# Down projection by seven products: another order of the products, one weight sum for each, and low parts on VectorE

## Chip, cores, metric

One core of one Trainium2 chip runs the whole kernel. The metric is device time in microseconds (us); the median of three runs is given. Numbers of the profile come from one profiled execution.

## The reference

One encoder layer over 1024 tokens of width 1024 in float32: a modulated norm, one input projection into an attention group and an mLSTM group, an output projection, then the feed-forward part with 2816 hidden units and a final norm. What matters here is the end:

```python
h = modulate(rms_norm(x, norm_ffn_g[l]), sh2, sc2)
ffn = (jax.nn.silu(h @ w_gate[l]) * (h @ w_up[l])) @ w_down[l]
x = x + g2[:, None, :] * ffn
...
return rms_norm(x, final_norm_g)
```

The change lies in `@ w_down[l]`, a product of 1024 x 2816 by 2816 x 1024.

## The kernel before

**Precision.** Each float32 operand is split into a high part (rounded to the type fp32r by ScalarE) and a low part (the operand minus its high part). A product is three matmuls, high by high, low by high, high by low (`mm3`, lines 312 to 314 of the profile).

**Seven products for eight.** Weights and activations are cut in halves in two directions, and the block product is made with seven products and some sums (Winograd's form of Strassen's scheme). The hidden units are 22 blocks of 128, taken as NP = 11 pairs `p`. `WD[c, p]` holds the rows of block 2p + c of `w_down`, 128 x 1024; its column halves give the weight quarters a11 = `WD[0, p]` left, a21 = `WD[0, p]` right, a12 = `WD[1, p]` left, a22 = `WD[1, p]` right. The activation side of each product `m` (11, 21, T2, T3, T1, 22, T4) has been summed already in the stage before and lies in DRAM as `act_d[p][m]`, 128 x 512. Product `m` runs over the 11 pairs; for each it multiplies one 128 x 512 weight piece (four output blocks of 128) with one activation piece, into four PSUM accumulators. T4 is done in two halves of 256 tokens. When a product ends, `finish` adds its four accumulators, scaled by the gate g2, into those quarters of the residual that the table `CELLS` names: four for 11, one for 21, three for T2, two each for T3 and T1, one each for 22 and T4, so 16, 4, 12, 8, 8, 4 and 4 (twice, half as wide) additions on VectorE. `FINAL` says after which product a quarter is complete, so that its squares for the final norm can be taken.

**Weight pieces.** `load_w` makes the weight piece of one product and pair, one call per pair, four ahead. For T2 it makes three sums: a11 - a21 in place of a11, s = a22 - a11 in a tile of its own, and, after the split, a12 - s in place of a12. T3 then finds its weight in a11 and 22 its own in a12; T1 adds a22 to a21 in place. The high part `wch` is ScalarE's, the low part `wcl` VectorE's, in four buffers each. T4's weight a22 is split into a tile `a`. The first KB = 5 pairs of product 11 load their weights as pieces instead (below).

**Pieces.** Activation pieces (and those five weight pieces) come through `load_piece`: SyncE issues a load into one of three buffers `wst`; ScalarE makes `whi`, then the engine chosen in `split` makes `wlo`; the buffer is free after that. `split` uses GpSimd (`gps`) unless `lo` names VectorE. In the down projection `lo` is `dve` only for the second half of T4. Loads, x and `wd` rows share SyncE's queue, which is served in order.

**Order.** Each engine runs its instructions in the order of the program. That order is made while the program is written out: `ck` is a model of the engines' times, in which a `chain` of steps puts each step behind what it waits for. VectorE's instructions for sums, low parts and accumulators so interleave as the model's times say.

Of the kernel before, what the change touches and what calls it, by code (L numbers as in the profile page):

```python
# [11 lines left out]
F32 = mybir.dt.float32  # L12
# [8 lines left out]
P = 128  # L21
# [3 lines left out]
HALF = 512  # L25
# [23 lines left out]
MIX = [("o", i) for i in range(16)] + [("m", (i + 8) % 16) for i in range(16)]  # L49
FF = [("b", p) for p in range(NB)] + [("v", 0)] + [("s", (p, i)) for p in range(1, NP - 1) for i in range(2)] + [("v", NP - 1)]  # L50
SET = ["A11", "A12", "S2", "S3", "S1", "A22", "S4"]
DOWN = ["11", "21", "T2", "T3", "T1", "22", "T4"]

VEC = {}
_o = 0
# [194 lines left out]
def layer_kernel(ctx, tc, xT, c, w_ada, vecs, cons, rope, w_f, w_fT, w_t0, w_t, w_o, w_gu, w_d, out):  # L250
# [43 lines left out]
    x1_d = [dram.tile([P, S], F32, name=f"x1_d{i}") for i in range(KT)]  # L294
    act_d = [{m: dram.tile([P, HALF], F32, name=f"act_d{p}{m}") for m in DOWN} for p in range(NP)]

# [24 lines left out]
    def halves(n):  # L321
        return slice(n * HALF, (n + 1) * HALF)

    ck = Clock()
    dve, act, gps = Engine(ck, nc.vector, "dve"), Engine(ck, nc.scalar, "act"), Engine(ck, nc.gpsimd, "gps")
# [39 lines left out]
    with tc.manual_schedule():  # L365
# [48 lines left out]
        def down_w():  # L414
            out = []
            for m in DOWN:
                for c in range(2 if m == "T4" else 1):
# [10 lines left out]
        specs = [first[f][b] for b in range(2) for f in range(3)]  # L428
        start = {("t", 0): [6, 8, 9, 11], ("q", 1): [7, 10]}
# [31 lines left out]
        def split(p, delay, src, shape, *before, lo=None):  # L461

            def split_hi():
                p[0] = lined("whi", shape)
                act.activation(p[0], src(), AF.Copy)

            def split_lo():
                p[1] = lined("wlo", shape)
                (lo or gps).tensor_sub(p[1], src(), p[0].bitcast(F32))

            ck.chain(delay, *before, split_hi, split_lo, flag=p[2])
# [3 lines left out]
        def piece(i):  # L475

            p = [None, None, Flag()]
            made.append((p, Flag(), []))
            if not isinstance(specs[i][0], str):
                src, n, ncol = specs[i][:3]  # L480

                def arrived(st, arrive):
                    made[i][2].append(st)
                    ck.chain(arrive, lambda: None, flag=made[i][1])

                raw([P, n, ncol], src, p[2], arrived)

        def load_piece():

            i = len(pieces)  # L490
            if i == len(specs):
                return
            while len(made) <= min(i + (AHEAD if i + AHEAD >= start["down"] else 0), len(specs) - 1):
                piece(len(made))
            p, there, st = made[i]
            pieces.append(p)
            if isinstance(specs[i][0], str):
                set_piece(p, *specs[i][1])
                return
            split(p, 0.0, lambda: st[0], [P, *specs[i][1:3]], there,  # L500
                  lo=dve if specs[i][3:] == (1,) or i < 9 or start["o", 0] <= i < start["b", 1] else None)

        def weights(w0, k, per):
            w = pieces[w0[k // per] if isinstance(w0, list) else w0 + k // per]
# [88 lines left out]
        def issue():  # L593

            kind, i = loads[0][0], int(loads[0][1:] or 0)
            del loads[0]
            if kind == "x":
                ck.chain(dma(x_t[i], xT[i]), lambda: None, flag=x_at[i])
            elif kind == "a":
                ada_load(i)  # L600
            else:
                load_piece()
            if loads:
                ck.at(max(0.0, ck.dma_t - 5.0 - ck.now), issue)
# [760 lines left out]
        HB, b22_ok, rs_used = {}, {}, []  # L1365
        hb_ok = {(m, k): Flag() for m in DOWN for k in range(4)}

# [84 lines left out]
        def set_piece(e, p, i, m):  # L1452

            s = 2 * p + i
            R, Q = RAW[s], set_s[s]
            set_p[s][m] = e[2]
            eng = dve if p == 0 else gps
            done = lambda x: [set_p[s][x]] if x in set_p[s] else []
            sh = [P, 4, P]
            if m[0] == "A":  # L1460
                split(e, 0.0, lambda: R[m[1:]][0], sh, R[m[1:]][1], lo=eng)
            elif m == "S2":
                split(e, 0.0, lambda: Q[2], sh, s2_ok[s], lo=eng)
            elif m == "S3":
                split(e, 0.0, lambda: R["11"][0], sh, s2_ok[s], *done("A11"),
                      lambda: dve.tensor_sub(R["11"][0], R["11"][0], R["21"][0]), lo=eng)
            elif m == "S1":
                split(e, 0.0, lambda: Q[1], sh, s2_ok[s], lo=eng)
            else:
                split(e, 0.0, lambda: R["12"][0], sh, s2_ok[s], R["12"][1], *done("A12"),  # L1470
                      lambda: dve.tensor_sub(R["12"][0], R["12"][0], Q[2]), lo=eng)
            if len(set_p[s]) == (7 if p >= NB else 5):
                ck.chain(0.0, *set_p[s].values(), lambda: None, flag=sets_done[s])
                if s + 2 < 2 * NP:
                    ck.chain(0.0, sets_done[s], lambda: load_raws(s + 2))
# [159 lines left out]
        def act_sums(p):  # L1635
# [6 lines left out]
            def new(m, a, b):  # L1642
# [9 lines left out]

        CELLS = {"11": ("11", "12", "21", "22"), "21": ("11",), "T2": ("12", "21", "22"), "T3": ("21", "22"),
                 "T1": ("12", "22"), "22": ("12",), "T4": ("21",)}
        FINAL = {"21": "11", "T1": "22", "22": "12", "T4": "21"}
        WD, wd_ok = {}, {(c, p): Flag() for c in range(2) for p in range(NP)}
        x1_ok = {(k, n): Flag() for k in range(KT) for n in range(NH)}
        wseq = [(m, c, p) for m in DOWN for c in range(2 if m == "T4" else 1) for p in range(NP)
                if m != "11" or p >= KB]
        WE = {q: [None, None, Flag()] for q in wseq}  # L1660
# [31 lines left out]
        def load_w():  # L1692
            if not wseq:
                return
            q = m, c, p = wseq.pop(0)
            e = WE[q]
            if m == "T4":
                if c == 0:
                    t = pb.tile([P, 2, HALF], F32R, tag=f"wd0{p}", name="a22")
                    e[:2] = t[:, 0], t[:, 1]  # L1700
                    WE[m, 1, p] = e
                    a22 = WD[1, p][:, halves(1)]
                    ck.chain(0.0, lambda: act.activation(t[:, 0], a22, AF.Copy),
                             lambda: dve.tensor_sub(t[:, 1], a22, t[:, 0].bitcast(F32)), flag=e[2])
                return
            a11, a12, a21, a22 = (WD[x, p][:, halves(r)] for r in range(2) for x in range(2))
            src = {"11": a11, "21": a12, "T3": a11, "T1": a21, "22": a12, "T4": a22}.get(m)
            ok = [wd_ok[x, p] for x in ((0,) if m in ("11", "T3") else (1,) if m in ("21", "22", "T4") else (0, 1))]
            steps, rest = [], []
            if m == "T2":  # L1710

                src = pb.tile([P, HALF], F32, tag="s", name="s", bufs=5)
                if ("11", 0, p) in WE:
                    ok.append(WE["11", 0, p][2])
                ok.append(WE["21", 0, p][2])
                steps = [lambda: dve.tensor_sub(a11, a11, a21), lambda: dve.tensor_sub(src, a22, a11)]
                rest = [lambda: dve.tensor_sub(a12, a12, src)]
            elif m in ("T3", "22"):
                ok.append(WE["T2", 0, p][2])
            elif m == "T1":  # L1720
                ok.append(WE["T3", 0, p][2])
                steps = [lambda: dve.tensor_add(a21, a21, a22)]
            eng = dve

            def hi():
                e[0] = pb.tile([P, HALF], F32R, tag="wch", name="wch", bufs=4)
                act.activation(e[0], src, AF.Copy)

            def lo():
                e[1] = pb.tile([P, HALF], F32R, tag="wcl", name="wcl", bufs=4)  # L1730
                eng.tensor_sub(e[1], src, e[0].bitcast(F32))

            ck.chain(0.0, *ok, *steps, hi, lo, *rest, flag=e[2])

        def down():
            i = start["down"]
            flat = lambda t: t.rearrange("p a b -> p (a b)")
            for m in DOWN:
                for c in range(2 if m == "T4" else 1):
# [28 lines left out]
        def finish(m, c, banks):  # L1768
            w = 256 if m == "T4" else HALF
            for o in range(4):  # L1770
# [11 lines left out]
                ck.chain(LAT, opened3, *steps, flag=f)  # L1782
                cell = FINAL.get(m)
                if cell in ("12", "22"):
# [476 lines left out]
        pb = ctx.enter_context(tc.tile_pool(name="pb", bufs=1))  # L2261
# [81 lines left out]
```

## Time and profile before

| | |
|---|---|
| median of 3 runs | 1366.47 us (1365.18 to 1368.64) |
| the profiled execution's own time | 1367.06 us |
| its span, first to last instruction | 1365.0 us |
| mean granted TensorE clock | 0.977 |
| TensorE busy | 1282.9 us, 94% |
| VectorE busy | 1052.8 us, 77% |
| ScalarE busy | 708.7 us, 52% |
| GpSimd busy | 644.5 us, 47% |
| down projection, first to last matmul start | 1123.74 to 1353.24 us |

In rows of the profile PE is TensorE, PEld its weight loads, DVE VectorE, ACT ScalarE, POOL GpSimd, SP SyncE. L98 is a helper's line through which all engine instructions pass, so tiles tell them apart, written out<-in. A busy TensorE is not a TensorE at full pace, since matmuls overlap; distances between starts tell more.

### The profile page before, as it was taken

Reading aid. Unit: us, or ns where it says so; the run is one execution under the profiler, and the core shown is the slowest. Engines: PE = TensorE matmul, PEld = TensorE weight load, DVE = VectorE, ACT = ScalarE, POOL = GpSimd, SP = SyncE. Lnnn points to the kernel's source line nnn. Section 1 sums busy time; section 2 is a strip of 40 time slices with the busy share of each in tenths; the row PEclk is TensorE's granted clock in tenths of the full one; section 3 lists DMA queues with packets and bytes.
Section 4 is the critical chain, followed back from the end, with each engine's and each line's share of the span. In section 5 each row is a group of like instructions: output and inputs, shape, how many; then the busy total and the mean of one; then the engine's idle time right before and its main releaser. Section 6 shows DMA issues by size and latency. Waiting matters only on the chain.

```text
span 1365.0 us, 19568 instructions
## 1 busy us (share of the span) xinstructions
PE 1282.9 (94%) x6596; PEld 1077.1 (79%) x6596; DVE 1052.8 (77%) x1601; ACT 708.7 (52%) x1342; POOL 644.5 (47%) x536
## 2 busy tenths in 40 slices
PE   7899888899999989999999999999999999979997
PEld 5787676888788979788778788888888887858887
DVE  7936698976689847989789989867666754898866
ACT  6575466778577855555577422333323334444462
POOL 0352577655665524444124155554545445545542
PEclk9888898999999999999999999999999999989999
DMA  9444333233233226773553344332333259623314
GB/s 360 159 122 138 113 103 97 78 104 110 67 92 103 76 83 192 235 248 109 186 178 115 99 144 150 118 108 100 109 107 116 72 187 347 252 80 104 100 59 158
DMA packets 104467, 187.02 MB, mean 137 GB/s; under 512 B 11568, under 2 KB 33200, under 8 KB 104368
## 3 DMA queue, kind: packets, MB, share of 16 engines
q1 hardware_dynamic: 90976, 163.68, 37.2%
q10 hardware_dynamic: 13392, 22.10, 4.3%
q8 instruction: 52, 0.85, 0.3%
q14 instruction: 47, 0.39, 0.1%
HBM read 139.33 MB, written 42.73 MB: 133 GB/s over the span
## 4 chain that ended last, share of the span: by engine, by line
PE 60%; DVE 18%; issue 7%; DMA 5%; ACT 5%; POOL 4%; SPq 1%; DVEq 0%; ACTq 0%; POOLq 0%
PE acc L312 16%; PE acc L314 16%; PE acc L313 16%; DVE sst L98 3%; DVE y L98 3%; DVE PT L98 2%; PE av L1210 2%; DVE x L98 2%; PE T L1191 2%; PE S L1159 1%; POOL wlo L98 1%; DMA wst<-act_d 1%; DMA wst<-in_w_gu_dram 1%; DVE wd L98 1%; DVE s L98 1%
## 5 line engine op out<-in xcount | busy, mean ns | idle before, releaser
L98 POOL TENSOR_TENSOR wlo<-wst,whi 128x512 fp32r<-128x512 f32 (+2 forms) x165 | 239.9, 1460 | 287.7 <-ACT whi L98 234.0
L98 ACT ACTIVATE whi<-wst 128x512 fp32r<-128x512 f32 (+2 forms) x223 | 133.6, 605 | 119.6 <-PE acc L314 28.3
L313 PE MATMUL acc<-x,whi 128*128 128x512 f32 x352 | 136.9, 389 | 0.0
L98 POOL TENSOR_SCALAR P<-P,sst 128x1024 f32<-128x1024 f32 x64 | 85.9, 1343 | 89.5 <-DVE sst L98 65.4
L98 POOL TENSOR_TENSOR wlo<-wr,whi 128x512 fp32r<-128x512 f32 x52 | 72.2, 1389 | 71.7 <-ACT whi L98 68.6
L312 PE MATMUL acc<-hh,whi 128*128 128x512 f32 x224 | 98.1, 438 | 6.9 <-ACT xp L98 5.2
L312 PE MATMUL acc<-whi,wch 128*128 128x512 f32 x244 | 96.0, 394 | 5.2 <-ACT wch L98 5.2
L314 PE MATMUL acc<-whi,wcl 128*128 128x512 f32 x244 | 96.5, 396 | 3.2 <-DVE wcl L98 3.2
L313 PE MATMUL acc<-wlo,wch 128*128 128x512 f32 x244 | 96.1, 394 | 0.5 <-POOL wlo L98 0.4
L98 ACT ACTIVATE P<-S,sst,colq 128x1024 f32<-128x1024 f32 x64 | 77.2, 1207 | 36.8 <-DVE sst L98 27.3
L313 PE MATMUL acc<-hl,whi 128*128 128x512 f32 x224 | 91.0, 406 | 0.0
L314 PE MATMUL acc<-hh,wlo 128*128 128x512 f32 x224 | 90.7, 405 | 0.0
L98 DVE TENSOR_TENSOR PT<-T,PT 128x512 fp32r<-128x512 f32 x128 | 83.3, 680 | 9.5 <-ACT PT L98 9.3
L98 ACT ACTIVATE whi<-wr 128x512 fp32r<-128x512 f32 x56 | 35.4, 632 | 100.1 <-DVE wr L98 48.3
L98 DVE TENSOR_REDUCE sst<-S 128x1 f32<-128x1024 f32 x64 | 77.7, 1213 | 12.5 <-PE S L1159 12.4
L1191 PE MATMUL T<-ident,P 128*128 128x128 f32 x512 | 72.6, 280 | 15.3 <-DVE PT L98 10.5
L98 ACT ACTIVATE PT<-T 128x512 fp32r<-128x512 f32 x128 | 71.7, 596 | 29.1 <-PE T L1191 28.3
L312 PE MATMUL acct<-whi,hh 128*128 128x256 f32 (+1 forms) x256 | 81.5, 318 | 4.5 <-ACT hh L98 3.1
L1191 PEld LDWEIGHTS T<-ident,P 128*128 128x128 f32 x512 | 59.3, 143 | 26.2 <-issue 9.7
L98 DVE TENSOR_TENSOR wcl<-wd,wch 128x512 fp32r<-128x512 f32 x50 | 50.0, 1012 | 37.9 <-ACT wch L98 29.4
L98 POOL TENSOR_TENSOR wlo<-s,whi 128x512 fp32r<-128x512 f32 x40 | 55.1, 1379 | 49.4 <-ACT whi L98 49.4
L1210 PE MATMUL av<-PT,va 128*128 128x256 f32 x512 | 71.4, 287 | 7.0 <-DVE PT L98 6.9
(486 smaller groups left out, 3849.4 us busy)
## 6 DMA issues: line engine op xcount, KB each, us to landing
wr<-in_w_gu_dram SPq DMA_DIRECT2D x66, 256.0 KB, 2.8
ada<-in_w_ada_dram SPq DMA_DIRECT2D x64, 256.0 KB, 3.4
wd<-in_w_d_dram SPq DMA_DIRECT2D x22, 512.0 KB, 6.7
wst<-in_w_gu_dram SPq DMA_DIRECT2D x42, 256.0 KB, 2.9
wst<-act_d SPq DMA_DIRECT2D x33, 256.0 KB, 4.4
ada<-in_w_ada_dram SPq DMA_DIRECT2D x16, 512.0 KB, 7.2
wst<-in_w_o_dram SPq DMA_DIRECT2D x32, 256.0 KB, 3.3
act_d<-sg ACTq DMA_DIRECT2D x29, 256.0 KB, 2.0
```

The source lines that it names most:

```text
L98: return fn(*args, **kw)
L312: nc.tensor.matmul(acc, w[0], x[0], start=first, stop=False)
L313: nc.tensor.matmul(acc, w[0], x[1], start=False, stop=False)
L314: nc.tensor.matmul(acc, w[1], x[0], start=False, stop=last)
L1159: nc.tensor.matmul(sp[:, halves(n)], qs[:, j * P:(j + 1) * P], k2[g][m][:, halves(n)], start=m == 0, stop=m == 1)
L1191: nc.tensor.transpose(tp[:, k], Pt[q][:, (4 * b + k) * P:(4 * b + k + 1) * P], ident)
L1210: nc.tensor.matmul(av, va[:, k, h // 4], PT[it][m][:, k], start=(k, m) == (0, 0), stop=(k, m) == (NJ - 1, 1))
```

## The change

The order of the products becomes 11, 21, T3, T1, T2, 22, T4. Each of T3, T1, T2 and 22 makes its weight by one sum in place: T3 a11 - a21 in a11; T1 a21 + a22 in a21; T2 a22 - a11 in a11 (after T3 is done with it); 22 a12 - a11 in a12 (after T2). The tile s goes. Quarter 22 is complete after T2. All low parts of pieces of the down projection are made by VectorE.

```diff
-DOWN = ["11", "21", "T2", "T3", "T1", "22", "T4"]
+DOWN = ["11", "21", "T3", "T1", "T2", "22", "T4"]
...
-                  lo=dve if specs[i][3:] == (1,) or i < 9 or start["o", 0] <= i < start["b", 1] else None)
+                  lo=dve if i >= start["down"] or i < 9 or start["o", 0] <= i < start["b", 1] else None)
...
-        FINAL = {"21": "11", "T1": "22", "22": "12", "T4": "21"}
+        FINAL = {"21": "11", "T2": "22", "22": "12", "T4": "21"}
...
-            src = {"11": a11, "21": a12, "T3": a11, "T1": a21, "22": a12, "T4": a22}.get(m)
+            src = {"11": a11, "21": a12, "T3": a11, "T1": a21, "T2": a11, "22": a12}[m]
             ok = [wd_ok[x, p] for x in ((0,) if m in ("11", "T3") else (1,) if m in ("21", "22", "T4") else (0, 1))]
-            steps, rest = [], []
-            if m == "T2":
-
-                src = pb.tile([P, HALF], F32, tag="s", name="s", bufs=5)
+            steps = []
+            if m == "T3":
                 if ("11", 0, p) in WE:
                     ok.append(WE["11", 0, p][2])
-                ok.append(WE["21", 0, p][2])
-                steps = [lambda: dve.tensor_sub(a11, a11, a21), lambda: dve.tensor_sub(src, a22, a11)]
-                rest = [lambda: dve.tensor_sub(a12, a12, src)]
-            elif m in ("T3", "22"):
-                ok.append(WE["T2", 0, p][2])
+                steps = [lambda: dve.tensor_sub(a11, a11, a21)]
             elif m == "T1":
                 ok.append(WE["T3", 0, p][2])
                 steps = [lambda: dve.tensor_add(a21, a21, a22)]
+            elif m == "T2":
+                ok.append(WE["T3", 0, p][2])
+                steps = [lambda: dve.tensor_sub(a11, a22, a11)]
+            elif m == "22":
+                ok += [WE["T2", 0, p][2], WE["21", 0, p][2]]
+                steps = [lambda: dve.tensor_sub(a12, a12, a11)]
...
-            ck.chain(0.0, *ok, *steps, hi, lo, *rest, flag=e[2])
+            ck.chain(0.0, *ok, *steps, hi, lo, flag=e[2])
```

More of the change, by code (lines that the diff above doesn't have):

```diff
@@ L1722, in load_w @@
                 steps = [lambda: dve.tensor_add(a21, a21, a22)]
-            eng = dve
+            elif m == "T2":
[4 more added lines that the diff above has]
+                steps = [lambda: dve.tensor_sub(a12, a12, a11)]
             def hi():
@@ L1730, in lo @@
                 e[1] = pb.tile([P, HALF], F32R, tag="wcl", name="wcl", bufs=4)
-                eng.tensor_sub(e[1], src, e[0].bitcast(F32))
-            ck.chain(0.0, *ok, *steps, hi, lo, *rest, flag=e[2])
+                dve.tensor_sub(e[1], src, e[0].bitcast(F32))
+            ck.chain(0.0, *ok, *steps, hi, lo, flag=e[2])
         def down():
```

## The prediction

> **What bounds the kernel now.** I read the page for the span, then the trace's busy time by stage with the cuts laid where TensorE begins a new product of the down projection (found in its timeline: 132 matmuls a product, 11 pieces x 4 output blocks x 3 terms; the last product has two halves of 132 narrower ones).
>
> ```profile
> span 1365.0 us, 19568 instructions
> ...
> core 0: us, PE busy (x) PEld busy (x) DVE busy (x) ACT busy (x) POOL busy (x), PEclk, DMA share, GB/s
> 1123.74:1156.05 32.31, 31.15 (x133) 24.40 (x132) 11.96 (x16) 13.28 (x21) 16.48 (x13) 1.00 0.92 328
> 1156.05:1186.34 30.29, 30.26 (x133) 24.66 (x132) 26.50 (x33) 13.88 (x23) 16.31 (x12) 1.00 0.83 320
> 1186.34:1227.88 41.54, 33.53 (x133) 25.43 (x132) 40.19 (x45) 18.56 (x34) 19.56 (x14) 0.92 0.27 77
> 1227.88:1258.88 31.00, 30.56 (x134) 24.63 (x132) 26.06 (x29) 12.72 (x22) 16.90 (x13) 1.00 0.38 110
> 1258.88:1288.80 29.92, 29.92 (x134) 24.78 (x132) 26.02 (x28) 12.82 (x22) 15.48 (x11) 1.00 0.33 97
> 1288.80:1318.72 29.92, 29.92 (x134) 24.78 (x132) 21.53 (x30) 16.31 (x31) 13.05 (x11) 1.00 0.23 68
> 1318.72:1335.40 16.68, 16.68 (x136) 16.20 (x135) 14.57 (x18) 10.99 (x22) 8.79 (x8) 1.00 0.26 85
> 1335.40:1353.24 17.84, 17.84 (x143) 17.58 (x142) 12.33 (x27) 5.62 (x15) 2.50 (x3) 1.00 0.63 207
> ```
>
> The rows are products 1 to 6 and the two halves of product 7. Products 5 and 6 run without a gap: 29.92 us, or 0.227 us a matmul. Against that, product 1 (11) loses 2.4 us, product 2 (21) 0.4, product 3 (T2) 11.6, product 4 (T3) 1.1: 15.5 us in all. That sum is the ceiling of what any relief of the feeding engines can give here. In product 3 VectorE is busy 40.19 of 41.54 us (97%) and the clock granted to TensorE falls to 0.92. TensorE's timeline shows how:
>
> ```profile
> 1194.28 0.39 PE L314 MATMUL acc<-whi,wcl 128*128 128x512 f32 x1
> 1198.85 0.50 PE L312 MATMUL acc<-whi,wch 128*128 128x512 f32 x1 [4.18 <-ACT wch L98]
> 1199.18 0.56 PE L313 MATMUL acc<-wlo,wch 128*128 128x512 f32 x1
> 1202.51 0.79 PE L314 MATMUL acc<-whi,wcl 128*128 128x512 f32 x1 [2.77 <-DVE wcl L98]
> 1203.10 0.63 PE L312 MATMUL acc<-whi,wch 128*128 128x512 f32 x1
> 1203.53 0.63 PE L313 MATMUL acc<-wlo,wch 128*128 128x512 f32 x1
> ```
>
> TensorE waits for the high part wch and then the low part wcl of one weight piece, and then goes on at 0.43 us a matmul, half its pace, for a while: the pause is paid twice. Behind wch stands VectorE, as the waits between engines and the groups of VectorE's instructions in product 3 say:
>
> ```profile
> ACT wch L98 <- DVE s L98: 25.5, 9, 4.2
> ...
> L98 DVE TENSOR_TENSOR s<-wd,wd 128x512 f32<-128x512 f32 x9 | 12.1, 1347 | 0.0
> L98 DVE TENSOR_TENSOR wd<-wd,s 128x512 f32<-128x512 f32 x10 | 8.9, 900 | 0.0
> L98 DVE TENSOR_TENSOR wcl<-s,wch 128x512 fp32r<-128x512 f32 x9 | 8.3, 926 | 1.2 <-ACT wch L98 1.2
> L98 DVE TENSOR_TENSOR wd<-wd 128x512 f32<-128x512 f32 x9 | 8.3, 925 | 0.0
> ```
>
> Three sums and one low part a piece, by those means 1.35 + 0.90 + 0.93 + 0.93 = 4.1 us, where TensorE needs 29.92/11 = 2.72 us a piece. VectorE is what product 3 is bound by. Why the same instruction costs 0.9 to 1.35 us on average is seen by laying its single rows beside GpSimd's:
>
> ```profile
> 1208.91 1.69 POOL L98 TENSOR_TENSOR wlo<-wst,whi 128x512 fp32r<-128x512 f32 x1 [1.82 <-ACT whi L98]
> 1214.28 1.29 POOL L98 TENSOR_TENSOR wlo<-wst,whi 128x512 fp32r<-128x512 f32 x1 [3.68 <-ACT whi L98]
> ...
> 1211.67 0.68 DVE L98 TENSOR_TENSOR wd<-wd,s 128x512 f32<-128x512 f32 x1
> 1212.28 0.68 DVE L98 TENSOR_TENSOR s<-wd,wd 128x512 f32<-128x512 f32 x1
> 1212.88 0.68 DVE L98 TENSOR_TENSOR wd<-wd 128x512 f32<-128x512 f32 x1
> 1214.32 1.80 DVE L98 TENSOR_TENSOR s<-wd,wd 128x512 f32<-128x512 f32 x1
> ```
>
> Between GpSimd's two low parts VectorE starts an instruction every 0.60 to 0.61 us (call it 0.605). The one that starts 0.04 us after GpSimd's at 1214.28 takes 1.80: it sat out the 1.29. The price of a VectorE instruction with two tile inputs is thus 0.605 us alone and up to 1.8 beside GpSimd.
>
> **The change, part by part.**
>
> *Low parts moved from GpSimd to VectorE.* Over products 1 to 7a:
>
> ```profile
> L98 POOL TENSOR_TENSOR wlo<-wst,whi 128x512 fp32r<-128x512 f32 x66 | 93.2, 1419 | 94.4 <-ACT whi L98 91.5 <-PE acc L314 2.6
> L98 POOL TENSOR_TENSOR wlo<-wst,whi 128x256 fp32r<-128x256 f32 x11 | 10.5, 962 | 8.5 <-ACT whi L98 8.5
> ...
> L98 DVE TENSOR_TENSOR wcl<-wd,wch 128x512 fp32r<-128x512 f32 x50 | 50.0, 1012 | 37.9 <-ACT wch L98 29.4 <-DMA wd<-in_w_d_dram 8.3
> ```
>
> GpSimd loses 93.2 + 10.5 us; beyond its two multiplications of the first closing norm nothing is left on it before 1335 us. VectorE gains 66 x 0.605 + 11 x about 0.35 (half width, half of 0.605 and a little) = 44 us, and should get back what it waits for GpSimd: of the 50 low parts in the last row alone 50 x (1.012 - 0.605 - the 0.08 by which a row's 0.68 overlaps the next start) = 16 us, and the sums and low parts of the group rows above (0.90 to 1.35) the like. So its total hardly moves; what matters is how it falls on the products.
>
> *One sum a product.* T2's three sums become one each in T3, T2 and 22, T1 keeps its own: 44 sums before and after. With the low parts, products 3 to 5 now ask VectorE for 33 instructions at 0.605 = 20.0 us, plus the additions out of the accumulators that the product before leaves. These are
>
> ```profile
> L98 DVE SCALAR_TENSOR_TENSOR x<-acc,mod,x 128x512 f32<-128x512 f32 x52 | 35.5, 737 | 0.7 <-PE acc L314 0.7
> ...
> 1155.74 4.04 DVE L98 SCALAR_TENSOR_TENSOR x<-acc,mod,x 128x512 f32<-128x512 f32 x6
> ```
>
> six in 4.04 us, about 0.66 apart (one tile input, the other in the accumulator; I see no such row stretched like the sums). In the order 11, 21, T3, T1, T2, 22 the products leave 16, 4, 8, 8, 12 and 4. VectorE's bill: product 2: 22 x 0.605 + 16 x 0.66 = 23.9 us; 3: 20.0 + 2.6 + three norm sums 1.8 = 24.4; 4 and 5: 20.0 + 5.3 = 25.3; 6: about 27 full instructions (7 sums, 7 low parts of 22, 8 of T4's weights, 5 of pieces) 16.3, 6 half ones 2.1, 12 additions 7.9, 3 norm sums 1.8 = 28.1; TensorE takes 29.92 each time. Before, VectorE at 26.06 and 26.02 us in products 4 and 5 cost TensorE little or nothing, so 24 to 25 should pass. Product 3 then goes from 41.54 to about 30.2: -11.3. Product 4, whose 1.1 us is the tail of the same backlog: -1.1. Product 6 is at 94%, with four weight pieces (10.9 us of TensorE) made ahead: I put +0.5, bounds 0 and +3. Product 7 (VectorE 14.57 of 16.68 in its first half; the half-width low parts add some 3 us, the low parts of T4's weights give as much back): +0.5, bounds 0 and +3.
>
> *Product 1.* Its stalls hang on GpSimd's low parts, which also free the three load buffers. The chain there, merged rows of which every other kind is left out:
>
> ```profile
> 1126.58 1.78 POOL wlo L98
> ...
> 1132.02 1.31 POOL wlo L98
> ...
> 1140.28 1.30 POOL wlo L98
> ...
> 1152.07 1.27 POOL wlo L98
> ...
> 1153.38 0.50 PE acc L313
> ```
>
> Four links of 1.3 to 1.8 us would be 0.7 each: up to 2.9 us sooner, of which 2.4 are TensorE's stall. But DMA is busy at 0.92 in product 1's row of the table, so part turns into waiting for loads: -1.4, bounds 0 and -2.4. VectorE's own queue costs nothing new here: ScalarE makes the high parts of both kinds in one queue already, so the low parts come in the order that VectorE now gets.
>
> *Product 2.* Here a cover goes. At 1153.38 TensorE takes a piece whose low part ended at that moment: the pieces have no lead. And 16 additions stand on VectorE from 1155.74, six in a row. GpSimd took a low part beside them:
>
> ```profile
> 1155.84 1.30 POOL L98 TENSOR_TENSOR wlo<-wst,whi 128x512 fp32r<-128x512 f32 x1 [1.26 <-ACT whi L98]
> ```
>
> On VectorE it can stand behind some of them: behind all six it would end at about 1160.4, where TensorE wants that piece (the second of the product) at 1156.05 + 2.72 = 1158.8, a stall of 1.6, and SyncE's load that waits for the buffer, with the weight rows queued behind it, starts 3.2 us later; two or three times over, 5 us. At best low parts get cheaper and the 0.4 goes: bounds -0.4 and +5. Up to four additions can be queued at one time, one per accumulator, so a wait of 1 to 2 us is nearer: +1.0.
>
> *No cost:* removing the tile s, the moved final cell 22 (still the fifth product's), the last product and the closing norm (same instructions, 11.8 us behind 1353.24).
>
> Sum: -1.4 + 1.0 - 11.3 - 1.1 + 0.5 + 0.5 = -11.8 us. The profiled execution took 1367.06 us (span 1365.0 and 2.06 around it), 0.6 above the median of 1366.47; the difference carries over: 1366.47 - 11.8 = 1354.7.
>
> **A rule weighed.** The Trainium skill, "Perfetto Trace Analysis", section Optimizing Scalar/DVE Operations, advises to take work off a saturated VectorE, even to GpSimd, and adds that between those two it may not help as they share a read port. By its first half, at the 97% of product 3, this change would go the wrong way; by its second it may pay. "SBUF — State Buffer", section Who interferes with whom, makes the second half definite: a VectorE instruction with two SBUF inputs and a GpSimd instruction that reads SBUF lock each other out for a whole instruction. The 1.80 us row beside GpSimd's 1.29 agrees; by it the sum is the -11.8 above, by the first half alone it is the second rival below.
>
> **The rivals.**
>
> *The second product pays.* The piece low parts stand behind the additions by their worst (+5), and products 6 and 7 cost +2 more than I put: -11.8 + 4 + 2, about 1360.5. For it: no lead, 16 additions, and loads that hang on the low part. Against: 23.9 of 29.92 us, and only TensorE's third product needs those accumulators.
>
> *VectorE becomes the bound (slower).* If the slow instructions are not GpSimd's doing, VectorE's prices stay at the means: 1.012 and 0.737. Then products 2 to 6 take 22 x 1.012 + 11.8 = 34.1; 36 x 1.012 + 2.9 = 39.3; twice 33.4 + 5.9 = 39.3; about 33 x 1.012 + 8.8 = 42.2: 194 us against 162.7 before, +31 less 1.4, about 1396. It decides at a mean of (162.7 - 48 x 0.66)/157 = 0.83 us for the 157 instructions; from there on the kernel is slower. Against: every run of 0.6 us starts lies where GpSimd is idle.
>
> *The stall only moves.* The third product waits for something else, the weight rows above all, of which the last are loaded late:
>
> ```profile
> wd<-in_w_d_dram SPq DMA_DIRECT2D x22, 512.0 KB, 6.7
> ...
> 1174.00 0.43 SPq L317 DMA_DIRECT2D wd<-in_w_d_dram  x1
> ```
>
> The last one lands near 1181, and it is for the fifth piece, due at 1186 + 4 x 2.72 = 1197: 16 us to spare. It would take all of that and more to eat the gain: 1366.
>
> **How the numbers follow.** A change within 0.3% (4.1 us, about what a measurement can tell here) is "same". Forecast, 1351 to 1358.5: 0.67. Second product pays, 1358.5 to 1362.4: 0.18. All 15.5 us gone, 1351.0 or less: 0.04. Stall moves: 0.06. VectorE the bound: 0.05. Faster 0.89, same 0.06, slower 0.05. The range 1351.0 to 1361 holds the forecast and most of the second case, 0.81.
>
> **What the profile after would show.** Right: no row of low parts on GpSimd in the down projection, VectorE's two-input means near 0.68 us, product 3 (now T3) near 30 us with granted clock 1.00, VectorE at 80 to 95% in products 2 to 6 all the same. Product 2 longer than 30.3 us with waits of TensorE for wlo: the second rival. Means above 0.83 us with GpSimd idle: the third. The prediction is wrong if weight pieces come late in product 3 though VectorE has idle time ahead of them, or if product 6 or 7 stalls by more than 3 us.

## The result, and the profile after

The changed kernel takes 1357.72 us (median of 8 runs, 1349.35 to 1361.06), the kernel before 1365.66 us (8 runs, 1361.64 to 1369.61): ratio 0.9933, 95% interval 0.9917 to 0.9949. It is faster by 0.7%, inside the range of the prediction, by 8 us where 11.8 were forecast.

The profiled execution took 1354.44 us, by the first line of its page with

```profile
span 1352.7 us, 19570 instructions
```

Its busy time by stage, cut again where TensorE begins a product (132 matmuls each, the last in two halves):

```profile
core 0: us, PE busy (x) PEld busy (x) DVE busy (x) ACT busy (x) POOL busy (x), PEclk, DMA share, GB/s
1119.56:1152.58 33.02, 30.64 (x133) 24.44 (x132) 18.22 (x28) 13.79 (x22) 0.00 (x0) 1.00 0.89 316
1152.58:1184.94 32.36, 30.34 (x133) 24.81 (x133) 28.23 (x46) 15.20 (x25) 0.00 (x0) 1.00 0.89 321
1184.94:1214.86 29.92, 29.92 (x134) 24.77 (x132) 25.26 (x42) 17.12 (x30) 0.00 (x0) 1.00 0.41 107
1214.86:1244.78 29.92, 29.92 (x134) 24.77 (x132) 25.67 (x43) 12.92 (x22) 0.00 (x0) 1.00 0.35 98
1244.78:1274.70 29.92, 29.92 (x134) 24.77 (x132) 25.67 (x43) 12.92 (x22) 0.00 (x0) 1.00 0.34 97
1274.70:1305.56 30.86, 30.25 (x134) 24.70 (x132) 30.20 (x52) 16.65 (x31) 0.00 (x0) 1.00 0.23 68
1305.56:1322.24 16.68, 16.68 (x136) 16.20 (x135) 12.81 (x23) 10.04 (x19) 2.62 (x2) 1.00 0.24 72
1322.24:1340.93 18.69, 18.60 (x143) 17.70 (x142) 13.71 (x28) 6.58 (x17) 3.27 (x4) 1.00 0.59 205
```

The third product, 41.54 us before, runs at TensorE's pace with the full granted clock. The fourth lost its 1.1 us. Products 1, 2, 6 and 7 are longer than before, by 0.7, 2.1, 0.9 and 0.9 us. From the first to the last matmul start the down projection takes 221.4 us against 229.5: 8.1 us less, close to the difference of the medians (7.9). The two profiled executions differ by more, 12.6 us, because the down projection began 4.2 us sooner in this one. That is not the change's doing: in the 14 profiled executions of this study it began anywhere from 1117.5 to 1124.4 us, and two more executions of this same kernel began it at 1122.1 and 1120.2.

VectorE's groups over products 1 to 7a, then all that GpSimd does there:

```profile
L98 DVE TENSOR_TENSOR wlo<-wst,whi 128x512 fp32r<-128x512 f32 x66 | 45.2, 688 | 23.2 <-ACT whi L98 22.7
L98 DVE TENSOR_TENSOR wcl<-wd,wch 128x512 fp32r<-128x512 f32 x61 | 41.5, 685 | 8.9 <-ACT wch L98 8.9
L98 DVE SCALAR_TENSOR_TENSOR x<-acc,mod,x 128x512 f32<-128x512 f32 x52 | 36.8, 743 | 0.0
L98 DVE TENSOR_TENSOR wd<-wd,wd 128x512 f32<-128x512 f32 x33 | 22.3, 684 | 0.0
...
L98 POOL TENSOR_TENSOR x<-x,ny 128x512 f32<-128x512 f32 x2 | 3.3, 1657 | 214.3 <-DMA wst<-act_d1T 214.3
```

The mean of a two-input instruction fell from 1.01 us (wcl) and up to 1.32 (sums) to 0.685. So VectorE runs 76 more instructions between the first and the last matmul start of the down projection (295 for 219), and yet its busy time there is 179.8 us against 179.2.

What products 1 and 2 lost is seen in TensorE's waits, in ScalarE's high parts of weights before them, and in VectorE's instructions at the seam between the two products:

```profile
1134.73 0.50 PE L312 MATMUL acc<-whi,wch 128*128 128x512 f32 x1 [1.41 <-ACT wch L98]
...
1152.58 0.50 PE L312 MATMUL acc<-whi,wch 128*128 128x512 f32 x1 [0.97 <-ACT wch L98]
1155.34 0.50 PE L314 MATMUL acc<-whi,wcl 128*128 128x512 f32 x1 [2.02 <-DVE wcl L98]
...
1134.05 0.63 ACT L98 ACTIVATE wch<-wd 128x512 fp32r<-128x512 f32 x1 [0.77 <-DMA wd<-in_w_d_dram]
...
1151.90 0.63 ACT L98 ACTIVATE wch<-wd 128x512 fp32r<-128x512 f32 x1 [0.57 <-DMA wd<-in_w_d_dram]
1151.96 2.72 DVE L98 SCALAR_TENSOR_TENSOR x<-acc,mod,x 128x512 f32<-128x512 f32 x4
1154.60 0.68 DVE L98 TENSOR_TENSOR wcl<-wd,wch 128x512 fp32r<-128x512 f32 x1
```

Both pauses of TensorE for wch (1.41 and 0.97 us) end at a high part that ScalarE could make only when its weight row had landed. The cuts lie at starts of matmuls, so both count to product 1. The first weights of product 2 come from a row that lands just before 1151.90. The high part is ready at 1152.5, but in VectorE's order four additions stand ahead of the low part, which waits until 1154.60: 2.02 us of TensorE's time, and almost all that product 2 lost. In the kernel before, TensorE's longest wait in product 1 was for GpSimd's low part, and VectorE made the first two low parts of product 2's weights ahead of the additions, which began at 1155.74:

```profile
1135.93 0.50 PE L314 MATMUL acc<-whi,wlo 128*128 128x512 f32 x1 [0.68 <-POOL wlo L98]
...
1153.88 1.94 DVE L98 TENSOR_TENSOR wcl<-wd,wch 128x512 fp32r<-128x512 f32 x2 [4.44 <-ACT wch L98]
```

### The profile page after: what moved, and what is told of

Its sections match the earlier page's. It is cut to its first block, busy times and chain, and to the rows that moved or that the text cites. A ratio compares the mean times of both kernels' runs of the same rounds, so it can differ in the third digit from the quotient of the medians.

```text
span 1352.7 us, 19570 instructions
## 1 busy us (share of the span) xinstructions
PE 1275.2 (94%) x6596; PEld 1072.6 (79%) x6596; DVE 1053.8 (78%) x1683; ACT 710.0 (52%) x1342; POOL 533.6 (39%) x454
## 4 chain that ended last, share of the span: by engine, by line
PE 61%; DVE 18%; issue 7%; DMA 5%; ACT 5%; POOL 3%; SPq 1%; DVEq 0%; ACTq 0%; POOLq 0%
PE acc L314 16%; PE acc L312 16%; PE acc L313 16%; DVE sst L98 3%; DVE x L98 2%; DVE y L98 2%; PE av L1210 2%; PE T L1191 2%; DVE PT L98 2%; PE S L1159 2%; SPq L317 1%; PE U L1917 1%; DVE wlo L98 1%; POOL wlo L98 1%; PE ni L2001 1%
## 5 line engine op out<-in xcount | busy, mean ns | idle before, releaser
L98 POOL TENSOR_TENSOR wlo<-wst,whi 128x512 fp32r<-128x512 f32 (+1 forms) x83 | 129.6, 1566 | 178.3 <-ACT whi L98 127.4
L98 DVE TENSOR_TENSOR wlo<-wst,whi 128x512 fp32r<-128x512 f32 (+2 forms) x140 | 93.2, 669 | 32.0 <-ACT whi L98 31.4
L98 POOL TENSOR_TENSOR x<-x,ny 128x256 f32<-128x256 f32 (+1 forms) x8 | 8.3, 1066 | 234.7 <-DMA wst<-act_d1T 214.3
L98 ACT ACTIVATE whi<-wr 128x512 fp32r<-128x512 f32 x56 | 35.4, 632 | 100.0 <-DVE wr L98 48.3
```

The source lines that it names most:

```text
L98: return fn(*args, **kw)
```

## The experiments

Lengths of the products in us, from the starts of matmuls 1, 133, 265 and so on in TensorE's timeline of each profile (the last column is the whole, first to last start):

| kernel | 1 | 2 | 3 | 4 | 5 | 6 | 7 | all |
|---|---|---|---|---|---|---|---|---|
| before | 32.3 | 30.3 | 41.5 | 31.0 | 29.9 | 29.9 | 34.5 | 229.5 |
| after | 33.0 | 32.4 | 29.9 | 29.9 | 29.9 | 30.9 | 35.4 | 221.4 |
| after, second time | 34.1 | 31.8 | 29.9 | 29.9 | 29.9 | 30.8 | 35.8 | 222.3 |
| after, third time | 33.1 | 32.4 | 29.9 | 29.9 | 29.9 | 30.8 | 36.6 | 222.7 |
| e1 order only | 31.1 | 29.9 | 30.3 | 35.4 | 35.8 | 36.8 | 34.5 | 233.8 |
| e2 low parts only | 33.4 | 32.4 | 33.4 | 29.9 | 29.9 | 29.9 | 35.5 | 224.4 |
| e3 low parts from product 3 on | 31.0 | 30.0 | 29.9 | 29.9 | 29.9 | 30.9 | 35.5 | 217.0 |
| e3, second time | 32.4 | 30.3 | 29.9 | 29.9 | 29.9 | 30.9 | 35.0 | 218.4 |
| e4 GpSimd reads beside | 34.7 | 33.3 | 34.8 | 38.9 | 37.8 | 41.9 | 36.0 | 257.4 |
| e5 rows on ScalarE's queue | 35.5 | 31.6 | 29.9 | 29.9 | 29.9 | 30.8 | 35.6 | 223.3 |
| e6 T4's first low parts on GpSimd | 32.7 | 30.1 | 29.9 | 29.9 | 29.9 | 30.8 | 35.5 | 218.9 |
| e7 T2 before T1 | 32.4 | 30.1 | 29.9 | 29.9 | 30.3 | 30.1 | 36.3 | 219.1 |
| e8 low parts from piece 11 | 32.2 | 31.8 | 29.9 | 29.9 | 29.9 | 30.9 | 35.9 | 220.5 |
| e9 low parts from product 2 | 30.9 | 35.3 | 29.9 | 29.9 | 29.9 | 30.9 | 35.8 | 222.6 |

For one kernel products 3 to 6 repeat within 0.1 us, product 1 within 1.5 us, product 2 within 0.6 us and product 7 within 1.3 us.

**The parts alone: e1 and e2.** My theory was that the third product was slow through four VectorE instructions a piece, so that the order alone would do; the rival, that GpSimd beside VectorE is what costs.

e1, on the kernel after:

```diff
-                  lo=dve if i >= start["down"] or i < 9 or ...
+                  lo=dve if specs[i][3:] == (1,) or i < 9 or ...
```

> The new order with one sum a product, but GpSimd keeps the low parts of pieces as before. Theory: the third product was slow because it asked VectorE for three sums and a low part a piece; one sum and one low part, even at the 1.0 us that they cost beside GpSimd, come to 2 us of 2.72, so products 3 to 6 run at 29.9 to 30.3 us. Products 1 and 2 stay as before (32.3 and 30.3), the last at 34.5: down projection about 217 us, against 229.5 before and 221.4 after, so this one beats the full change by 4 to 5 us. Rival (the low parts on VectorE are what pays, since GpSimd no longer stretches its instructions): the third product stays at 34 us or more and the whole is slower than after.

e2, on the kernel before:

```diff
-                  lo=dve if specs[i][3:] == (1,) or i < 9 or ...
+                  lo=dve if i >= start["down"] or i < 9 or ...
```

> The old order with the three sums in T2, but all low parts of pieces on VectorE. Theory: T2 asks VectorE for five instructions a piece, 55 x 0.605 = 33.3 us, and 4.5 us of additions and norm sums: the third product takes 34 to 38 us, against 41.5 before; products 1 and 2 are as after (33.0 and 32.4), down projection about 226 us. Rival (the move of the low parts is what pays): the third product is near 30 us.

e1: 1369.84 us, ratio to before 1.0037 (1.002 to 1.0053): slower by 0.4%. e2: 1360.08 us, 0.9965 (0.9946 to 0.9984). My theory missed on e1: the third product did fall to 30.3 us by the order alone, but products 4 to 6, which I had put at 29.9 to 30.3, took 35.4 to 36.8. The rival had the time right, slower than after, and the place wrong. Product 4 of e1 by stage:

```profile
1212.75:1248.17 35.42, 31.74 (x134) 24.15 (x132) 29.96 (x32) 12.71 (x23) 15.30 (x12) 1.00 0.30 91
```

VectorE's groups in it (busy, mean ns, idle before):

```profile
L98 DVE TENSOR_TENSOR wd<-wd,wd 128x512 f32<-128x512 f32 x12 | 18.1, 1511 | 0.0
L98 DVE TENSOR_TENSOR wcl<-wd,wch 128x512 fp32r<-128x512 f32 x12 | 9.9, 822 | 6.2 <-ACT wch L98 6.2
```

And its timeline: VectorE, GpSimd, and a pause of TensorE:

```profile
1215.69 0.69 DVE L98 TENSOR_TENSOR wcl<-wd,wch 128x512 fp32r<-128x512 f32 x1 [0.76 <-ACT wch L98]
1216.30 1.79 DVE L98 TENSOR_TENSOR wd<-wd,wd 128x512 f32<-128x512 f32 x1
1218.85 0.69 DVE L98 TENSOR_TENSOR wcl<-wd,wch 128x512 fp32r<-128x512 f32 x1 [0.76 <-ACT wch L98]
1219.46 1.79 DVE L98 TENSOR_TENSOR wd<-wd,wd 128x512 f32<-128x512 f32 x1
1221.17 3.37 DVE L98 SCALAR_TENSOR_TENSOR x<-acc,mod,x 128x512 f32<-128x512 f32 x5
1224.47 1.14 DVE L98 TENSOR_TENSOR wcl<-wd,wch 128x512 fp32r<-128x512 f32 x1
...
1216.25 1.29 POOL L98 TENSOR_TENSOR wlo<-wst,whi 128x512 fp32r<-128x512 f32 x1 [1.87 <-ACT whi L98]
1219.41 1.29 POOL L98 TENSOR_TENSOR wlo<-wst,whi 128x512 fp32r<-128x512 f32 x1 [1.87 <-ACT whi L98]
...
1225.67 0.50 PE L314 MATMUL acc<-whi,wcl 128*128 128x512 f32 x1 [2.91 <-DVE wcl L98]
```

VectorE is busy 30 of 35.4 us, 85%, not full. But the sum of the next piece starts 0.05 us after GpSimd's low part, in one piece after the other, and waits it out: 1.79 us instead of 0.68. Then ScalarE makes wch, then VectorE wcl, then comes the next sum: one piece every 3.16 us (1215.69 to 1218.85) where TensorE needs 2.72. The lead of up to four pieces shrinks by 0.44 us a piece. Then five additions (3.37 us) come ahead of the wcl of 1224.47, the lead no longer covers them, and TensorE stops; the kernel after has the same 8 additions in product 4 and no pause. So it is not VectorE's total that bounds these products but a chain of three steps, with the additions on top. The order needs GpSimd out of the way, and low parts without the order leave 33.4 us in the third product (e2, by stage):

```profile
1189.38:1222.78 33.40, 30.91 (x133) 24.55 (x132) 33.40 (x56) 17.34 (x30) 0.00 (x0) 1.00 0.32 100
```

There VectorE is busy 33.40 of 33.40 us with 56 instructions, 0.60 us apart: the bound by sheer number that five instructions a piece give. That is the mechanism of my theory; the time lies just under its 34 to 38 us. The two parts do not add up: +4.3 and -5.1 us of the down projection alone, -8.1 together.

**GpSimd beside VectorE: e4.** After each full low part GpSimd subtracts the two parts once more into a tile that nobody reads, which leaves VectorE's work and order as they are:

```diff
                 (lo or gps).tensor_sub(p[1], src(), p[0].bitcast(F32))
+                if JUNK and shape[1] == 4:
+                    nc.gpsimd.tensor_sub(JUNK[0], p[0].bitcast(F32), p[1].bitcast(F32))
```

> The full change, and GpSimd subtracts the two parts of each 512-wide piece once more into a tile that nobody reads (from the tenth piece or so on), so that its two-input instructions lie beside VectorE again with VectorE's work unchanged. Theory (the two lock each other out): VectorE's mean for two-input instructions rises from 0.68 to 0.9 us or more, and products 4 to 6 lengthen from 29.9 and 30.9 to 33 to 39 us. Rival (VectorE was slow for another reason): means stay at 0.68 and the products at 29.9 and 30.9.

1392.01 us in one run; products 4 to 6 at 37.8 to 41.9, the last of them beyond my 39. VectorE's groups in product 4:

```profile
L98 DVE TENSOR_TENSOR wcl<-wd,wch 128x512 fp32r<-128x512 f32 x12 | 16.8, 1401 | 1.0 <-ACT wch L98 1.0
L98 DVE TENSOR_TENSOR wd<-wd,wd 128x512 f32<-128x512 f32 x11 | 11.5, 1042 | 0.0
L98 DVE TENSOR_TENSOR wlo<-wst,whi 128x512 fp32r<-128x512 f32 x11 | 7.5, 678 | 0.0
L98 DVE SCALAR_TENSOR_TENSOR x<-acc,mod,x 128x512 f32<-128x512 f32 x8 | 5.7, 737 | 0.0
```

wcl, which follows the low part and so meets GpSimd, goes to 1.40 us, the sums to 1.04; wlo itself, which GpSimd waits for, stays at 0.68, and the additions out of PSUM at 0.74. In the trace of products 4 to 6, wcl and the sums take 1.34 and 1.41 us where they lie beside a GpSimd instruction and 0.68 where they do not; the additions take 0.74 in both places. VectorE runs the same instructions in the same order as in the kernel after, and is busy 116.0 us in these three products instead of 81.5. So the cause is shown: GpSimd's instruction beside it, not VectorE's own load. Whether GpSimd's reads or its writes do it e4 cannot tell, as its instruction does both. The Trainium skill, in "SBUF — State Buffer", Who interferes with whom, says that a VectorE instruction with two SBUF inputs contends with GpSimd's reads and not with its writes, and that one with at most one SBUF input is not touched, outside the modes that use both ports. These rows agree as far as they go, down to the additions, which have one input in SBUF.

**Products 1 and 2: e3, e5, e8, e9.** e3 gives GpSimd back the 27 pieces of these two products.

```diff
-                  lo=dve if i >= start["down"] or i < 9 or ...
+                  lo=dve if i >= start["down"] + 27 or i < 9 or ...
```

> The full change, but GpSimd keeps the low parts of the 27 pieces of products 1 and 2. Theory (what products 1 and 2 lost comes from the low parts on VectorE there, by the order of loads and by the queue): products 1 and 2 go back to 32.3 and 30.3 us, the third stays at 29.9, down projection about 218 us, 3 us under after. Rival (they lost by the new order of the products or by chance): they stay at 33.0 and 32.4.

1353.29 us, ratio 0.9921 (0.989 to 0.9952), and the products as the theory said or a little shorter: 31.0, 30.0, 29.9. The four executions with VectorE's low parts in products 1 and 2 (after three times, e2) took 33.0 to 34.1 and 31.8 to 32.4 us there; the six with GpSimd's (before, e1, e3 twice, e6, e7) 31.0 to 32.7 and 29.9 to 30.3. (e4 and e5, which change more, took 34.7 and 35.5, and 33.3 and 31.6.) The loss is tied to the low parts. How, was the next question. SyncE's queue around the first two loads of weight rows, in the kernel after:

```profile
1124.93 5.25 SPq L317 DMA_DIRECT2D wst<-act_d  x3
1130.36 0.81 SPq L317 DMA_DIRECT2D wd<-in_w_d_dram  x2
```

And before:

```profile
1131.44 0.32 SPq L317 DMA_DIRECT2D wst<-act_d  x1
1132.02 0.81 SPq L317 DMA_DIRECT2D wd<-in_w_d_dram  x2
```

In the kernel after, three piece loads stand there in a row, which wait for buffers for 5 us, and the rows leave 10.8 us behind the start of product 1 (1119.56); before, 8.3 us behind it (1123.74). In the written order the first rows stand behind 13 piece loads, before behind 11: the model of the engines' times knows that a low part is cheaper on VectorE, so it gives buffers free sooner and writes more piece loads ahead of the rows. e5 takes the rows out of that queue:

```diff
-                ck.chain(dma(new(), src), lambda: None, flag=f)
+                ck.chain(dma(new(), src, nc.scalar if f in wd_ok.values() else None), lambda: None, flag=f)
```

> The full change, with the 22 loads of weight rows (wd) issued from ScalarE's queue, so that on SyncE's queue they no longer stand behind piece loads that wait for a buffer. Theory: the pauses of product 1 for wch (1.8 and 1.4 us) and the start of product 2 come from weight rows that land late because of that queue: products 1 and 2 fall to about 31 and 30 us, down projection near 218 us. Rival (VectorE's queue is what is too full there: 16 additions and both kinds of low parts): product 1 keeps about 33, product 2 stays at 31.5 to 32.4.

1358.91 us, 0.9951 (0.9934 to 0.9969). Product 1 took 35.5 us, neither my 31 nor the rival's 33; product 2 took 31.6, the rival's. ScalarE in product 1 of e5, then ScalarE and VectorE at the seam to product 2:

```profile
1128.95 0.85 ACTq L317 DMA_DIRECT2D wd<-in_w_d_dram  x2
1134.08 0.63 ACT L98 ACTIVATE whi<-wst 128x512 fp32r<-128x512 f32 x1 [4.51 <-DMA wst<-act_d]
1134.61 1.13 ACT L98 ACTIVATE wch<-wd 128x512 fp32r<-128x512 f32 x2
...
1151.32 1.14 ACT L98 ACTIVATE wch<-wd 128x512 fp32r<-128x512 f32 x2
...
1152.06 2.72 DVE L98 SCALAR_TENSOR_TENSOR x<-acc,mod,x 128x512 f32<-128x512 f32 x4
1154.70 0.68 DVE L98 TENSOR_TENSOR wcl<-wd,wch 128x512 fp32r<-128x512 f32 x1
```

In product 1 ScalarE stands 4.51 us at a high part whose piece is still loading, and the two wch behind it then follow without a wait of their own: their rows were there, and ScalarE's order held them up. TensorE pauses 3.60 us for the first. So e5 doesn't tell what late rows cost product 1. Of product 2 it tells something: the first high part is ready when the additions begin at 1152.06, and still the first wcl comes behind four of them, since VectorE's order is written so. e8 and e9 restore the place of the rows by leaving GpSimd the first 10 or all 16 pieces of product 1 (`start["down"] + 10`, `+ 16` in the line of e3), with VectorE's low parts in product 2 as in the kernel after.

> The full change, but GpSimd makes the low parts of the first 10 pieces of the down projection. VectorE makes all others, those of the second half of product 1 and of product 2 among them, beside the 16 additions. By this the written order of SyncE's loads is again nearly that of before: the first two weight rows stand behind 11 pieces and not behind 13. Theory (the pauses of products 1 and 2 come from rows that stand too late in the written order of loads): product 1 falls to 31 to 32.5 us, product 2 to 30 to 30.5; down projection 217 to 219 us. Rival (VectorE's queue, with low parts of pieces among 16 additions, is the cause): product 2 stays at 31.5 to 32.4.

> As that, with GpSimd making the low parts of all 16 pieces of product 1; VectorE makes those of product 2. The rows stand early in the order of loads. Theory: products 1 and 2 at 31 to 32.5 and 30 to 30.5 us. Rival: product 2 stays at 31.5 to 32.4.

e8: 1354.79 us, 0.9911 (0.9892 to 0.9931); e9: 1356.95 in one run. Product 1: 32.2 and 30.9, as the place of the rows says. Product 2: 31.8 and 35.3; the first is what the rival said, the second is worse than that. e9 at the start of product 2, TensorE, ScalarE and VectorE:

```profile
1160.96 0.57 PE L313 MATMUL acc<-wlo,wch 128*128 128x512 f32 x1 [3.36 <-DVE wlo L98]
...
1155.00 1.28 ACT L98 ACTIVATE whi<-wst 128x512 fp32r<-128x512 f32 x2
...
1155.78 0.69 DVE L98 TENSOR_TENSOR wcl<-wd,wch 128x512 fp32r<-128x512 f32 x1
1156.38 1.41 DVE L98 SCALAR_TENSOR_TENSOR x<-acc,mod,x 128x512 f32<-128x512 f32 x2
1157.70 0.69 DVE L98 TENSOR_TENSOR wcl<-wd,wch 128x512 fp32r<-128x512 f32 x1
1158.30 0.75 DVE L98 SCALAR_TENSOR_TENSOR x<-acc,mod,x 128x512 f32<-128x512 f32 x1
1158.96 0.69 DVE L98 TENSOR_TENSOR wcl<-wd,wch 128x512 fp32r<-128x512 f32 x1
1159.56 0.75 DVE L98 SCALAR_TENSOR_TENSOR x<-acc,mod,x 128x512 f32<-128x512 f32 x1
1160.22 0.69 DVE L98 TENSOR_TENSOR wlo<-wst,whi 128x512 fp32r<-128x512 f32 x1
```

The high parts of two pieces are there by 1156.3. VectorE first makes three low parts of weights, with additions between them, and comes to the first wlo at 1160.22, 4 us later. Product 2's loss is VectorE's queue at the 16 additions. Which low part is late differs: wcl in the kernel after, wlo in e8 and e9. For product 1 the place of the rows fits all runs that load them from SyncE's queue: in the eight with 11 pieces ahead the first row leaves 8.2 to 8.4 us behind the start of product 1, which takes 30.9 to 32.7 us; in the five with 13 ahead (the kernel after three times, e2, e4) it leaves 10.8 to 11.5 us behind it, and the product takes 33.0 to 34.7. But GpSimd's pieces there change with the place of the rows, and no run moves the rows alone. What is left of the loss in e8 (a pause of 1.0 us for wch) stays open.

**Products 6 and 7: e6 and e7,** both on e3.

```diff
-                  lo=dve if i >= start["down"] + 27 or i < 9 or ...
+                  lo=dve if start["down"] + 27 <= i < start["down"] + 71 or i >= start["down"] + 82 or i < 9 or ...
```

> Low parts on VectorE for products 3 to 6 and the second half of 7 only; GpSimd keeps products 1 and 2 and the 11 half-wide pieces of the first half of 7. Theory (the 1 us that product 7 lost is the half-wide low parts on VectorE among the closing norm's work): product 7 goes from 35.5 back to 34.5, products 1 and 2 at 31.0 and 30.0; product 6, in which those half pieces are made, 30.9 or up to 2 us more as GpSimd's reads come back beside VectorE: down projection about 216 to 218 us. Rival: product 7 stays at 35.4.

1354.06 us, 0.9909 (0.9889 to 0.9928). Product 7 stayed at 35.5 (its first half longer, its second shorter): the theory fell. Product 1 took 32.7 us and not the 31.0 that I expected. What lengthens product 7 by 0.5 to 2.1 us stays open; in the third execution of the changed kernel, where it is longest, 1.22 us of its second half are a wait of TensorE for a high part whi, where the kernel before waits for none.

```diff
-DOWN = ["11", "21", "T3", "T1", "T2", "22", "T4"]
+DOWN = ["11", "21", "T3", "T2", "T1", "22", "T4"]
...
-        FINAL = {"21": "11", "T2": "22", "22": "12", "T4": "21"}
+        FINAL = {"21": "11", "T1": "22", "22": "12", "T4": "21"}
```

> As the version with GpSimd's low parts in products 1 and 2, but in the order 11, 21, T3, T2, T1, 22, T4: T2's 12 additions fall into the fifth product instead of the sixth, T1's 8 into the sixth. Theory (product 6 lost 0.94 us to VectorE at 98%, 12 additions and T4's weights): product 6 falls to 29.9, and the fifth, with 20.0 + 7.9 = 27.9 us of VectorE, stays at 29.9 to 30.3. Rival (product 6's stall is T4's weights alone): it keeps 0.9.

1354.70 us, 0.991 (0.9887 to 0.9932). Product 6 falls from 30.9 to 30.1 and the fifth rises to 30.3: the 12 additions cost what they were blamed for, but 0.4 of it moves with them.

**The same kernels again.**

> The changed kernel itself once more, to see what of a profile repeats. If the lengths of the products are the program's and the 4 us by which the down projection began earlier are the execution's, the products come out within 0.3 us of 33.0, 32.4, 29.9, 29.9, 29.9, 30.9 and 35.4, while the start of the down projection moves by some us.

> The changed kernel again, timed on the chip and in the rounds of the next one: about 0.993 of before, as on record; products 1 and 2 at 33 to 34 and 32 us.

> GpSimd's low parts in products 1 and 2, VectorE's from the third on, again: about 0.991 of before, 3 to 5 us under the changed kernel, with the down projection near 217 us.

r_after: 1357.9 us in one run. The start of the down projection moved by 2.6 us and products 3 to 6 came out as before, but products 1, 2 and 7 did not stay within 0.3 us (34.1, 31.8 and 35.8): their lengths are not the program's alone. The last two ran on one chip in the same rounds: after 1356.68, 0.9938 (0.9914 to 0.9962), e3 1353.58, 0.9905 (0.9885 to 0.9924). e3 beats both kernels, before by 0.8 to 1% in time and after by 4 us in the profiles (217.0 and 218.4 against 221.4 to 222.7). In times alone the intervals of after and e3 overlap, though in the shared rounds all four runs of e3 (1351.41 to 1355.95) lie below all four of after (1356.1 to 1361.33).

## Why the prediction was right, point by point

- Third product: -11.3 forecast, -11.6 measured, and for the reason given. VectorE's bill of 24.4 us was 25.26, and 0.685 us an instruction where 0.68 was read off the rows before. What the prediction did not split: by e1 the order alone gives 11.3 us of it in this product, and the move of the low parts is what then keeps products 4 to 6 at TensorE's pace.
- Fourth product: -1.1 as forecast. Fifth: nothing, as forecast.
- Contention, on which the slower rival turned: settled by e4. The rival's threshold missed something, though. It set GpSimd's cost against VectorE's total (a mean of 0.83 us); e1, with fewer instructions on VectorE, shows products slowed with VectorE at 85%, by the chain sum, high part, low part and the additions on top.
- Product 1: -1.4 forecast, +0.7 measured, and +0.8 to +1.8 in two more executions. This step failed. I argued that the order of the low parts follows ScalarE's order and costs nothing. But the order of SyncE's loads is written by the same model, and it changed: the change was not the same program with one engine exchanged. TensorE's two pauses for wch, 1.41 us within the product and 0.97 us at the seam, are for rows that landed late.
- Product 2: +1.0 forecast, +2.1 measured (+1.5 and +2.1 again). The kind of wait was named, a low part behind the 16 additions, and its size was taken as 1 to 2 us and entered at the lower end; it was 2.0. But the low part was the wrong one: the prediction looked for waits for a piece's wlo, and TensorE waited for a weight's wcl behind four additions. wlo was late only in e8 and e9.
- Product 6: +0.5 forecast, +0.9 measured; VectorE's bill 28.1, measured 30.20 of 30.86 us. Product 7: +0.5 forecast, +0.9 measured and up to +2.1 in other executions; not explained.
- The sum: -11.8 forecast, -8.1 in the products. Of the 3.7 us between them 2.1 are product 1, 1.1 product 2, 0.4 each products 6 and 7, less 0.3 in product 3. The time, 1357.72, lies as near to the rival in which the second product pays (about 1360.5) as to the forecast's 1354.7, though product 1, on which the rival says nothing, is the largest part of the miss. That it lies inside the forecast's 1351 to 1358.5 is in part luck: the kernel before came out at 1365.66 us in these rounds, 0.8 us under the 1366.47 from which the forecast was reckoned, and 7.9 us off the latter would have been 1358.5, the very edge.

## What to carry to other kernels

Work that goes to an idle engine is not free when the two engines lock each other out: here GpSimd's 1.3 us per piece stretched VectorE's instructions by about the 0.6 us that the same work costs on VectorE, since VectorE's busy time stayed at 179 to 180 us. What the change gained lies in where that time falls. Where a scheduler with a cost model writes the order, a cheaper instruction moves loads and other queues too; compare the written order of every queue, not only the engine's. And move work stage by stage: the low parts pay in products 3 to 6, and cost in 1 and 2, where VectorE has a burst of additions and the loads are tight.

## What the runs showed of the hardware that I had not expected

- An engine that isn't full can still set the pace through the lock. In e1 GpSimd's start and the sum's start fell into step, 0.05 us apart, one piece after the other (1216.25 and 1216.30, 1219.41 and 1219.46), for most pieces of products 4 and 5, since both hang on ScalarE's two high parts that follow each other.
- A pause of TensorE is not always paid twice. In e1 three pauses of 3.30 us from start to start lay at 1222.4, 1257.5 and 1292.4 us. After the first the matmuls went on at 0.23 us; after the other two six or more in a row ran at 0.43. The granted clock over the products in which the pauses lie is 1.00, 0.95 and 0.95. In the second execution of the changed kernel a pause of 2.50 us was followed by 0.43, in its first one of 2.42 us was not. The Trainium skill, "TensorE: Matmul & The Clock Gate", What's actually happening, says that the gate watches TensorE in windows that run free of the kernel. By that the same pause could fall into one window or be cut by two; no run here tests it. The same section of the Trainium skill puts the fall of the clock at an idle window of about 3.4 us; here a pause of 2.50 us from start to start was enough, and the measurement decides.
